# A first mixer whose small tables come through ScalarE's queue into tiles of their own, with constant products while x comes

## Chip, cores and metric

The kernel runs on one core of a Trainium2 chip, in one launch. The metric is the device time of a launch in microseconds: the median of the timed runs. A profiled execution of the kernel before is the source of every row below.

## What is computed

Four transformer layers on 256 tokens of width 1024, in float32, one batch. The first block has a layer with two causal depthwise convolutions as its mixer and a layer with stick-breaking attention, each followed by a mixture of 32 experts; the second block has two attention layers, each with a dense feed-forward part. What the change touches is the mixer of the first layer and what comes before it:

```python
def conv_mixers(x, w_in, conv_a, conv_b_w, conv_b_bias, norm_b_g, norm_b_b, w_out):
    u = jnp.einsum("bsd,de->bse", x, w_in)
    a_b, a_c, a_v, b_val, b_gate = jnp.split(u, [...], axis=-1)
    y_a = a_b * causal_depthwise_conv(a_c * a_v, conv_a)
    g = b_val * jax.nn.sigmoid(b_gate)
    g = causal_depthwise_conv(g, conv_b_w) + conv_b_bias
    y_b = jax.nn.silu(layer_norm(g, norm_b_g, norm_b_b))
    return jnp.einsum("bse,ed->bsd", jnp.concatenate([y_a, y_b], axis=-1), w_out)
...
x = layer_norm(DEEPNORM_ALPHA * x + mix, ln_mix_g[layer], ln_mix_b[layer])
ffn = hierarchical_moe(x, router_group_w[layer], ..., expert_w_up[layer], expert_w_down[layer])
```

## The kernel before

The program is one sequence of instructions per engine, in the order in which the code issues them; nothing reorders them. `T` is TensorE (PE in the rows), `V` VectorE (DVE), `S` ScalarE (ACT), `G` GpSimd (POOL) and `Q` SyncE (SP), which issues the loads of weights.

Weights are taken as items of 1 MB, each a tile of 128 x 2048 floats, in a fixed list: first the nine items of `even_w_in`, then `even_w_out`, then the experts'. `pump` (line 192 on) issues loads on SP's queue as long as a buffer is free; seven buffers belong to the pool `wa`, others are lent by stages. An item is used in two halves. For a product in full precision a half is split into two parts: ScalarE rounds it (`wh`, line 237) and VectorE subtracts (`wl`, line 248); when both halves of an item are split, its buffer is free and `pump` runs again. The two parts lie in pools of four buffers each, so a split can't run more than four halves ahead of TensorE. `mm3` (lines 396 to 399) makes three products of the parts. `tick` after each half runs work that `later` has put off by so many halves.

At the start `load_x` (line 296) and line 303 load x in two pieces of 128 tokens, and item 0 in two pieces between them. Line 202, in `pump`, loads the later items. `conv_mix` (line 540) then does, in this order: it issues the loads of the convolution's rows (lines 551 to 555: three rows of `even_conv_a`, 31 of `even_conv_b_w`, three of one row each) into `fvr`, seven loads of two rows each into `vr` (`vector_loads`, line 324), both of which are parts of one tile `scr`, and four loads for the router (lines 718 to 722); between them `pump` issues items. TensorE turns x piece by piece (`turned`, line 507), ScalarE rounds it (line 579), VectorE subtracts (line 580), both into `xh` and `xl`. Then the units of products begin: the first unit's first half is the opening (line 409), 24 products, whose first eight need only the rounded parts; its second half and all later halves are 24 products at lines 397 to 399. After the first unit (two halves) `vecs` (line 586) turns `fvr`, one half later `vectors` (line 331) turns `vr`. `tap_rows`, `tap_diag`, `shifted` and `conv` make the long convolution out of products.

Loads that SP and ScalarE issue each raise one of eight completion semaphores, DMAHW0 to DMAHW7. The framework hands these out in turn, over the two queues together, and a load that takes a semaphore again waits on its engine until the load that had it before is complete.

Of the kernel before, what the change touches and what calls it, by code (L numbers as in the profile page):

```python
# [10 lines left out]
F32 = mybir.dt.float32  # L11
# [9 lines left out]
SEQ = 256  # L21
# [44 lines left out]
def rows(ap):  # L66
    return ap.rearrange("(k p) n -> p k n", p=128)
# [3 lines left out]
def tile_kernel(ctx: ExitStack, tc: tile.TileContext, A, out, first=0, last=9):  # L71
# [12 lines left out]
    def bank():  # L84
        return psum.tile([128, 512], F32, name="ps", tag="ps")
# [230 lines left out]

    fvec = const.tile([128, 8, 14], F32, name="fvec")

    def vector_loads(vr):
        lo, hi = (0 if first < 4 else 8), (14 if last > 3 else 8)  # L320
        for j, n in enumerate(("ln_mix_g", "ln_mix_b", "ln_ffn_g", "ln_ffn_b", "norm_mix_2", "norm_ffn_2",
                               "norm_ple_2")):
            if lo <= 2 * j < hi:
                Q.dma_start(vr[2 * j:2 * j + 2, :], A[n])
        if lo:
            V.memset(vr[0:8, :], 0.0)

        def go():
            ps = bank()
            for k in range(8):  # L330
                T.transpose(ps[:, k * 14:k * 14 + hi], vr[0:hi, k * 128:(k + 1) * 128], ident[:hi, :hi])
            V.tensor_copy(fvec[:, :, 0:hi], ps[:, 0:112].rearrange("p (k n) -> p k n", k=8)[:, :, 0:hi])
        return go
# [206 lines left out]
    def conv_mix():  # L540


        with tc.tile_pool(name="cm", bufs=1, reuse_waits="tile") as cp:
            wd = [c_tile(F32).rearrange("p (n f) -> p n f", f=32) for _ in range(2)]
            xh, xl = take_c(2)
            scr = cp.tile([128, 2048], F32, name="scr")
            fvr, vr = scr[0:37, 0:512], scr[0:14, 1024:2048]
            yb = scr[:, 1024:2048].rearrange("p (b t) -> p b t", b=4)
            sq = scr[:, 0:1024].rearrange("p (b t) -> p b t", b=4)
            pump(2)  # L550
            Q.dma_start(fvr[0:3, :], A["even_conv_a"][0])
            Q.dma_start(fvr[3:34, :], A["even_conv_b_w"][0])
            Q.dma_start(fvr[34:35, :], A["even_conv_b_bias"])
            Q.dma_start(fvr[35:36, :], A["even_norm_b_g"])
            Q.dma_start(fvr[36:37, :], A["even_norm_b_b"])
            pump(1)
            vectors = vector_loads(vr)
            prep = router_loads(0)
            pump()
            vec = cp.tile([128, 4, 37], F32, name="vec")  # L560
            o512 = cp.tile([128, 128], F32, name="o512")
            G.memset(o512, 1.0 / 512)


            gp = cp.tile([128, 2, 32 + SEQ], F32, name="gp")
            gs = cp.tile([128, 2, 4, 28 + SEQ], F32, name="gs")
            ap = cp.tile([128, 2, 2 + SEQ], F32, name="ap")
            G.memset(gp[:, :, 0:30], 0.0)
            G.memset(gp[:, :, 30 + SEQ:], 0.0)
# [5 lines left out]
            for c in range(2):  # L575
                for kq in range(2):
                    v = turned(c, kq)
                    s = (slice(None), slice(4 * kq, 4 * kq + 4), slice(c * 128, (c + 1) * 128))
                    S.activation(xh[s], v, AF.Copy)
                    V.tensor_tensor(out=xl[s], in0=v, in1=xh[s].bitcast(F32), op=OP.subtract)  # L580
                split_to(c + 1)

            def vecs():
                ps = bank()
# [19 lines left out]

            def shifted():

                for b in range(2):
                    ps = [bank()[:, 0:28 + SEQ] for _ in range(4)]
                    for s in range(4):
                        for c in range(4):  # L610
                            f = slice(32 * c, 32 * c + 32)
                            T.matmul(ps[c][32 * s:32 * s + 32], ident[f, f], gp[f, b, s:s + 28 + SEQ], start=True,
                                     stop=True)
                    for c in range(4):
                        if c % 2:
                            S.activation(gs[:, b, c, :], ps[c], AF.Copy)
                        else:
                            V.tensor_copy(gs[:, b, c, :], ps[c])

            def conv(i):  # L620
                ps = bank()
                for b in range(2):
                    for q in range(8):
                        for c in range(4):
# [23 lines left out]
            nc.scalar.preload_act_table_set("silu_and_others")  # L648


            kept = {}

            def b_sum():
                m = bank()
                for b in range(4):
                    T.matmul(m[:, :256], o512, yb[:, b, :], start=b == 0, stop=b == 3)
                for b in range(4):
                    V.tensor_tensor(out=yb[:, b, :], in0=yb[:, b, :], in1=m[:, :256], op=OP.subtract)
                    S.activation(sq[:, b, :], yb[:, b, :], AF.Square)

            def b_stats():
                p2 = bank()
                for b in range(4):
                    for c in range(2):
                        T.matmul(p2[:, c:c + 1], sq[:, b, c * 128:(c + 1) * 128], o512[:, 0:1],
# [45 lines left out]

    rt = {}

    def router_loads(layer):

        mp = rt["pool"]
        rw = mp.tile([128, 8, 36], F32, name="rw")
        Q.dma_start(rw[:, :, 0:4], rows(A["router_group_w"][layer]))
        Q.dma_start(rw[:, :, 4:36], rows(A["router_expert_w"][layer]))
        lgc = mp.tile([1, 36], F32, name="lgc")  # L720
        Q.dma_start(lgc[:, 0:4], flat(A["router_group_b"][layer], 0, [[0, 1], [1, 4]]))
        Q.dma_start(lgc[:, 4:36], flat(A["router_expert_b"][layer], 0, [[0, 1], [1, 32]]))

        def go():
            ps = bank()
# [1292 lines left out]
```

## Time and profile before

| | us |
|---|---|
| median of 3 runs | 1921.65 |
| lowest and highest | 1921.64, 1921.94 |
| profiled execution | 1918.91 |
| its span | 1917.3 |
| TensorE busy | 1631.0 (85%) |
| VectorE busy | 738.6 (39%) |
| ScalarE busy | 676.8 (35%) |

The span is the time between the first and the last instruction of the profiled execution. TensorE's busy time counts instructions that wait in its pipeline, so it isn't a measure of peak use. In 40 slices of the span the DMA engines are full in two long stretches, the expert stages, and partly idle in the stages with dense products.

### The profile page before, as it was taken

The page shows a single profiled execution, that of the slowest core. Times are in us where ns is not written, and L with a number is a line of the kernel's source. Part 1 is how long each engine was busy: PE and PEld are TensorE (multiplying, and loading weights), DVE is VectorE, ACT ScalarE, POOL GpSimd, SP SyncE. Part 2 cuts the span into 40 slices and gives each one's busy share as a digit, 9 for nine tenths or more (in the row PEclk, how much of TensorE's full clock was granted, in tenths as well). Part 3 has the DMA queues.
Part 4 walks back from the last instruction along what each step waited for, and adds up shares of the span by engine and source line. Part 5 has one row for each costly group of instructions (what it writes and reads, how often), then busy time and mean ns, then how long its engine had stood idle before and what let it go on. Part 6 is the DMA issues. An engine that isn't in the chain of part 4 may idle for free. (4 is left out here: it accounts for less than half of the span.)

```text
span 1917.3 us, 35268 instructions
## 1 busy us (share of the span) xinstructions
PE 1631.0 (85%) x15117; PEld 1228.9 (64%) x15117; DVE 738.6 (39%) x1503; ACT 676.8 (35%) x1297; POOL 122.0 (6%) x126
## 2 busy tenths in 40 slices
PE   8999667677679998767667669999999998999998
PEld 7875323233238985323224227999999996799998
DVE  5551000001005661001001005666656857666557
ACT  4422111111116643111111114655444645654445
POOL 0010000000001000000000002101000412210002
PEclk9999878777789999878778789999999998999999
DMA  9689999999999469999999998545555463145550
GB/s 295 239 306 416 419 418 418 420 419 418 417 406 360 162 257 396 418 419 419 418 419 419 417 419 272 173 138 172 190 194 177 143 202 100 56 156 196 183 176 23
DMA packets 236571, 559.07 MB, mean 292 GB/s; under 512 B 15563, under 2 KB 124938, under 8 KB 236408
## 3 DMA queue, kind: packets, MB, share of 16 engines
q1 hardware_dynamic: 226520, 551.59, 75.2%
q10 hardware_dynamic: 9264, 4.97, 0.9%
q8 instruction: 122, 2.00, 0.4%
q14 instruction: 41, 0.34, 0.0%
q0 software_dynamic: 624, 0.18, 0.0%
HBM read 555.55 MB, written 1.15 MB: 290 GB/s over the span
## 5 line engine op out<-in xcount | busy, mean ns | idle before, releaser
L904 PE MATMUL ps<-w,xg 128*32 128x256 f32 x4096 | 365.0, 496 | 233.3 <-DMA w<-in_expert_w_up_dram 232.1
L904 PEld LDWEIGHTS ps<-w,xg 128*32 128x32 f32 x4096 | 136.1, 132 | 444.2 <-DMA w<-in_expert_w_up_dram 264.1
L248 DVE TENSOR_TENSOR wl<-w,wh 128x1024 fp32r<-128x1024 f32 x255 | 310.1, 1228 | 171.6 <-ACT wh L237 167.4
L237 ACT ACTIVATE wh<-w 128x1024 fp32r<-128x1024 f32 x273 | 283.1, 1051 | 91.5 <-PE ps L398 60.3
L908 DVE TENSOR_TENSOR hs<-hs,ps 128x128 f32<-128x128 f32 x64 | 18.4, 288 | 632.4 <-ACT hs L907 632.4
L397 PE MATMUL ps<-xh,wh 128*128 128x256 f32 (+1 forms) x840 | 237.1, 282 | 0.0
L399 PE MATMUL ps<-xh,wl 128*128 128x256 f32 (+1 forms) x840 | 236.3, 281 | 0.8 <-DVE wl L248 0.8
L398 PE MATMUL ps<-xl,wh 128*128 128x256 f32 (+1 forms) x840 | 236.6, 282 | 0.3 <-DVE xl L1229 0.3
L907 ACT ACTIVATE hs<-ps 128x128 f32<-128x128 f32 x64 | 17.8, 277 | 591.8 <-PE ps L904 587.2
L399 PEld LDWEIGHTS ps<-xh,wl 128*128 128x128 f32 (+1 forms) x840 | 159.2, 190 | 1.2 <-DVE wl L248 1.2
L398 PEld LDWEIGHTS ps<-xl,wh 128*128 128x128 f32 (+1 forms) x840 | 159.2, 190 | 1.1 <-DVE xl L1229 1.1
L397 PEld LDWEIGHTS ps<-xh,wh 128*128 128x128 f32 (+1 forms) x840 | 159.3, 190 | 0.0
L926 PE MATMUL ps<-w,ht 128*32 128x256 f32 x2048 | 142.2, 425 | 0.4 <-DMA w<-in_expert_w_down_dram 0.4
L933 ACT ACTIVATE y<-ps 32x256 f32<-32x256 f32 x256 | 95.8, 374 | 118.5 <-PE ps L926 111.6
L926 PEld LDWEIGHTS ps<-w,ht 128*32 128x32 f32 x2048 | 73.6, 127 | 67.6 <-issue 33.9
L399 PE MATMUL ps<-wh,xl 128*128 128x256 f32 x352 | 100.9, 287 | 4.5 <-DVE xl L1229 4.5
L397 PE MATMUL ps<-wh,xh 128*128 128x256 f32 x352 | 103.1, 293 | 1.5 <-ACT xh L1226 1.5
L248 POOL TENSOR_TENSOR wl<-w,wh 128x1024 fp32r<-128x1024 f32 x18 | 43.4, 2416 | 942.3 <-ACT wh L237 463.4
L398 PE MATMUL ps<-wl,xh 128*128 128x256 f32 x352 | 100.6, 286 | 0.0
L398 PE MATMUL ps<-al,wh 128*128 128x256 f32 x352 | 99.1, 281 | 0.0
L397 PE MATMUL ps<-ah,wh 128*128 128x256 f32 x352 | 99.1, 281 | 0.0
L399 PE MATMUL ps<-ah,wl 128*128 128x256 f32 x352 | 99.0, 281 | 0.0
(400 smaller groups left out, 2756.3 us busy)
## 6 DMA issues: line engine op xcount, KB each, us to landing
w<-in_expert_w_up_dram SPq DMA_DIRECT2D x256, 1024.0 KB
w<-in_expert_w_down_dram SPq DMA_DIRECT2D x128, 1024.0 KB
w<-in_w_ffn_gate_dram SPq DMA_DIRECT2D x22, 1024.0 KB
w<-in_w_ffn_up_dram SPq DMA_DIRECT2D x22, 1024.0 KB
w<-in_w_ffn_down_dram SPq DMA_DIRECT2D x22, 1024.0 KB
w<-in_odd_w_qkv_dram SPq DMA_DIRECT2D x12, 1024.0 KB
w<-in_w_in_ab_dram SPq DMA_DIRECT2D x12, 1024.0 KB
w<-in_w_in_nsa_dram SPq DMA_DIRECT2D x10, 1024.0 KB
```

What stands on the lines that cost most here:

```text
L237: S.activation(hv, src, AF.Copy)
L248: eng.tensor_tensor(out=lv, in0=src, in1=hv.bitcast(F32), op=OP.subtract)
L397: T.matmul(ps, lh, rh, start=start, stop=False, **kw)
L398: T.matmul(ps, lh, rl, start=False, stop=False, **kw)
L399: T.matmul(ps, ll, rh, start=False, stop=stop, **kw)
L904: T.matmul(pu[32 * j:32 * j + 32, 0:256], r, w[:, kk, :, j, :], start=k == 0, stop=k == 7)
L907: S.activation(hs, pu[:, 0:128], AF.Silu)
L908: V.tensor_tensor(out=hs, in0=hs, in1=pu[:, 128:256], op=OP.mult)
L926: T.matmul(pd[32 * c:32 * c + 32, 0:256], hts[e][:, 32 * j:32 * j + 32], w[:, jj, c * 256:(c + 1) * 256], start=j == 0, stop=j == 3)
L933: S.activation(y4s[q][32 * ee:32 * ee + 32, c * 256:(c + 1) * 256], pd[32 * c:32 * c + 32, 0:256], AF.Copy)
```

## The change

The loads of the small tables get an engine as a parameter, ScalarE, and stand together ahead of the first items that `pump` issues; the parts of `scr` become tiles of their own (`yb`, `fvr`, `vr`; `gs` and `sq` take the places of `fvr` and `vr` later on). ScalarE loads the table of the sigmoid once, behind these issues, in place of a first table at once and the sigmoid's later. `warm(n)` issues n products of 128 x 512 on a constant tile: eight before x, three between its two pieces.

```diff
-    def vector_loads(vr):
+    def vector_loads(vr, eng=Q):
...
-                Q.dma_start(vr[2 * j:2 * j + 2, :], A[n])
+                eng.dma_start(vr[2 * j:2 * j + 2, :], A[n])
...
-            scr = cp.tile([128, 2048], F32, name="scr")
-            fvr, vr = scr[0:37, 0:512], scr[0:14, 1024:2048]
-            yb = scr[:, 1024:2048].rearrange("p (b t) -> p b t", b=4)
-            sq = scr[:, 0:1024].rearrange("p (b t) -> p b t", b=4)
-            pump(2)
-            Q.dma_start(fvr[0:3, :], A["even_conv_a"][0])
...
-            Q.dma_start(fvr[36:37, :], A["even_norm_b_b"])
-            pump(1)
-            vectors = vector_loads(vr)
-            prep = router_loads(0)
+            yb = cp.tile([128, 4, SEQ], F32, name="yb")
+            fvr = cp.tile([37, 512], F32, name="fvr", tag="gs")
+            vr = cp.tile([14, D], F32, name="vr", tag="sq")
+            S.dma_start(fvr[0:3, :], A["even_conv_a"][0])
...
+            S.dma_start(fvr[36:37, :], A["even_norm_b_b"])
+            vectors = vector_loads(vr, S)
+            prep = router_loads(0, S)
+            nc.scalar.preload_act_table_set("sigmoid_and_others")
             pump()
+            warm(8)
...
                 split_to(c + 1)
+                if not c:
+                    warm(3)
...
+                gs = kept["gs"] = cp.tile([128, 2, 4, 28 + SEQ], F32, name="gs")
...
+                sq = kept["sq"] = cp.tile([128, 4, SEQ], F32, name="sq")
...
-    def router_loads(layer):
+    def router_loads(layer, eng=Q):
...
-        Q.dma_start(rw[:, :, 0:4], rows(A["router_group_w"][layer]))
-        Q.dma_start(rw[:, :, 4:36], rows(A["router_expert_w"][layer]))
+        eng.dma_start(rw[:, :, 0:4], rows(A["router_group_w"][layer]))
+        eng.dma_start(rw[:, :, 4:36], rows(A["router_expert_w"][layer]))
```

How the instructions stand on ScalarE at the start of the program, before the change; in brackets the semaphores on which an instruction waits (`w<-ps` is the rounding of x into `xh`, `wh<-w` that of a weight half):

```order
L579 ACT_TABLE_LOAD
L579 ACTIVATE w<-ps 128x4x128 [waits PE_49] x2
L237 ACTIVATE wh<-w 128x1024 [waits DMAHW1_49]
L579 ACTIVATE w<-ps 128x4x128 [waits PE_49] x2
L237 ACTIVATE wh<-w 128x1024 [waits DMAHW3_49]
L237 ACTIVATE wh<-w 128x1024 [waits DMAHW4_49]
L237 ACTIVATE wh<-w 128x1024
L237 ACTIVATE wh<-w 128x1024 [waits DMAHW5_49,DVE_49,PE_49]
L640 ACT_TABLE_LOAD
L640 ACTIVATE sg<-ps 128x512 [waits PE_49]
```

ScalarE issues no load here, and the rounding of x follows the first table load. In the changed kernel ScalarE's order is this, from the last loads of norm rows on (ahead of them stand the other eleven small loads):

```order
L324 DMA vr<-in_norm_ple_dram 2x1024 [waits DMAHW2_49]
L719 DMA rw<-in_router_group_w_dram 128x8x4 [waits DMAHW3_49]
L720 DMA rw<-in_router_expert_w_dram 128x8x32 [waits DMAHW4_49]
L722 DMA lgc<-in_router_group_b_dram 1x4 [waits DMAHW6_49]
L723 DMA lgc<-in_router_expert_b_dram 1x32 [waits DMAHW7_49]
L556 ACT_TABLE_LOAD
L578 ACTIVATE w<-ps 128x4x128 [waits PE_49] x2
L237 ACTIVATE wh<-w 128x1024
L578 ACTIVATE w<-ps 128x4x128 [waits PE_49] x2
L237 ACTIVATE wh<-w 128x1024 [waits DMAHW1_49]
L237 ACTIVATE wh<-w 128x1024 x2
L237 ACTIVATE wh<-w 128x1024 [waits DVE_49,PE_49]
```

All sixteen small loads stand ahead of the table load and of the rounding of x; the roundings of items 1 and 2 (the last two rows) have no wait for a load any more.

On SP's queue at the start of the program, before the change (the first `w` loads are the pieces of item 0, then items 1 and 2, and later item 3):

```order
L296 DMA x<-in_x_dram 128x1024
L303 DMA w<-in_even_w_in_dram 128x8x128
L296 DMA x<-in_x_dram 128x1024
L303 DMA w<-in_even_w_in_dram 128x8x128
L202 DMA w<-in_even_w_in_dram 128x8x256 x2
L551 DMA scr<-in_even_conv_a_dram 3x512
L552 DMA scr<-in_even_conv_b_w_dram 31x512
L553 DMA scr<-in_even_conv_b_bias_dram 1x512 [waits DMAHW0_49]
L554 DMA scr<-in_even_norm_b_g_dram 1x512 [waits DMAHW1_49]
L555 DMA scr<-in_even_norm_b_b_dram 1x512 [waits DMAHW2_49]
L202 DMA w<-in_even_w_in_dram 128x8x256 [waits DMAHW3_49]
L324 DMA scr<-in_ln_mix_g_dram 2x1024 [waits DMAHW4_49]
```

The first six loads wait for nothing, and the small loads stand between items 2 and 4. SP's queue in the changed kernel (the loads at line 202 are items 1, 2, 3 and so on):

```order
L296 DMA x<-in_x_dram 128x1024
L303 DMA w<-in_even_w_in_dram 128x8x128
L296 DMA x<-in_x_dram 128x1024
L303 DMA w<-in_even_w_in_dram 128x8x128 [waits DMAHW1_49]
L202 DMA w<-in_even_w_in_dram 128x8x256 [waits DMAHW3_49]
L202 DMA w<-in_even_w_in_dram 128x8x256 [waits DMAHW6_49]
L202 DMA w<-in_even_w_in_dram 128x8x256 [waits DMAHW1_49]
L202 DMA w<-in_even_w_in_dram 128x8x256 [waits DMAHW5_49]
L202 DMA w<-in_even_w_in_dram 128x8x256 [waits DMAHW0_49]
```

The small loads are gone from SP's queue, all nine items follow each other, and from the second piece of item 0 on each load waits for an earlier one, item 1 on DMAHW3 and item 2 on DMAHW6.

## Rows read from the trace of the kernel before

**Rows 1.** The page's head: the span of the profiled execution.

```profile
span 1917.3 us, 35268 instructions
```

**Rows 2.** Two stretches: us, busy time of each engine, granted clock, DMA share, GB/s.

```profile
core 0: us, PE busy (x) PEld busy (x) DVE busy (x) ACT busy (x) POOL busy (x), PEclk, DMA share, GB/s
60.00:80.00 20.00, 20.00 (x233) 16.67 (x233) 7.54 (x14) 5.67 (x11) 1.62 (x1) 1.00 0.50 189
300.00:400.00 100.00, 65.60 (x692) 30.08 (x694) 6.80 (x21) 14.26 (x39) 0.00 (x0) 0.81 1.02 419
```

**Rows 3.** SP's waits, 0 to 150 us: us in total, times, longest.

```profile
SPq L202 <- DVE wl L248: 56.7, 9, 18.2
...
SPq L324 <- DMA w<-in_even_w_in_dram: 2.3, 2, 1.3
```

**Rows 4.** TensorE's weight loads in time: start, us, line, count, idle time before them.

```profile
8.13 1.57 PEld L507 LDWEIGHTS ps<-ident,x 128*128 128x128 f32 x8 [1.77 <-DMA x<-in_x_dram]
9.94 1.79 PEld L409 LDWEIGHTS ps<-w,wh 128*128 128x128 f32 x8 [0.23 <-ACT w L579]
11.61 1.82 PEld L409 LDWEIGHTS ps<-w,wl 128*128 128x128 f32 x8
...
14.68 0.19 PEld L397 LDWEIGHTS ps<-w,wh 128*128 128x128 f32 x1
...
17.36 0.19 PEld L399 LDWEIGHTS ps<-w,wl 128*128 128x128 f32 x1
19.06 0.33 PEld L586 LDWEIGHTS ps<-ident,scr 37*128 37x128 f32 x4 [1.51 <-DMA scr<-in_norm_mix_dram]
...
22.89 0.57 PEld L331 LDWEIGHTS ps<-ident,scr 14*128 14x128 f32 x8 [0.59 <-DMA scr<-in_norm_mix_dram]
```

**Rows 5.** The same view at the opening of the attention stage.

```profile
588.05 1.05 PEld L409 LDWEIGHTS ps<-w,wh 128*128 128x128 f32 x8 [2.39 <-ACT w L1103]
589.04 1.00 PEld L409 LDWEIGHTS ps<-w,wl 128*128 128x128 f32 x8
```

**Rows 6.** ScalarE in time, 0 to 17 us.

```profile
0.91 1.28 ACT L579 ACT_TABLE_LOAD   x1 [0.91 <-PEq L2004]
5.95 0.60 ACT L579 ACTIVATE w<-ps 128x512 fp32r<-128x512 f32 x1 [3.76 <-PE ps L507]
...
9.29 0.60 ACT L579 ACTIVATE w<-ps 128x512 fp32r<-128x512 f32 x1 [0.94 <-PE ps L507]
10.14 0.60 ACT L579 ACTIVATE w<-ps 128x512 fp32r<-128x512 f32 x1 [0.26 <-PE ps L507]
10.64 1.05 ACT L237 ACTIVATE wh<-w 128x1024 fp32r<-128x1024 f32 x1
12.88 2.01 ACT L237 ACTIVATE wh<-w 128x1024 fp32r<-128x1024 f32 x2 [1.20 <-DMA w<-in_even_w_in_dram]
15.98 1.06 ACT L237 ACTIVATE wh<-w 128x1024 fp32r<-128x1024 f32 x1 [1.08 <-DMA w<-in_even_w_in_dram]
```

**Rows 7.** SP's queue in time, 12 to 24 us: start and duration of an issue.

```profile
12.88 1.68 SPq L324 DMA_DIRECT2D scr<-in_ln_mix_g_dram  x1
15.88 0.23 SPq L324 DMA_DIRECT2D scr<-in_ln_mix_b_dram  x1
...
22.53 0.43 SPq L721 DMA_DIRECT2D lgc<-in_router_group_b_dram  x1
23.01 0.25 SPq L722 DMA_DIRECT2D lgc<-in_router_expert_b_dram  x1
23.30 14.04 SPq L202 DMA_DIRECT2D w<-in_even_w_in_dram  x6
```

**Rows 8.** A stretch by engines, columns as in rows 2.

```profile
19.50:29.30 9.80, 9.38 (x83) 9.05 (x82) 8.22 (x15) 4.04 (x10) 0.00 (x0) 1.00 0.65 172
```

**Rows 9.** Stretches of half a microsecond by engines, columns as in rows 2.

```profile
22.50:23.00 0.50, 0.08 (x3) 0.11 (x2) 0.00 (x0) 0.50 (x1) 0.00 (x0) 1.00 0.59 18
23.00:23.50 0.50, 0.50 (x9) 0.47 (x9) 0.00 (x0) 0.50 (x2) 0.00 (x0) 1.00 1.14 114
23.50:24.00 0.50, 0.50 (x5) 0.50 (x5) 0.38 (x2) 0.50 (x1) 0.00 (x0) 1.00 1.17 192
```

More of the change, by code (lines that the diff above doesn't have):

```diff
@@ L545, in conv_mix @@
             xh, xl = take_c(2)
-            scr = cp.tile([128, 2048], F32, name="scr")
-            fvr, vr = scr[0:37, 0:512], scr[0:14, 1024:2048]
-            yb = scr[:, 1024:2048].rearrange("p (b t) -> p b t", b=4)
-            sq = scr[:, 0:1024].rearrange("p (b t) -> p b t", b=4)
-            pump(2)
-            Q.dma_start(fvr[0:3, :], A["even_conv_a"][0])
-            Q.dma_start(fvr[3:34, :], A["even_conv_b_w"][0])
-            Q.dma_start(fvr[34:35, :], A["even_conv_b_bias"])
-            Q.dma_start(fvr[35:36, :], A["even_norm_b_g"])
-            Q.dma_start(fvr[36:37, :], A["even_norm_b_b"])
-            pump(1)
-            vectors = vector_loads(vr)
-            prep = router_loads(0)
+            yb = cp.tile([128, 4, SEQ], F32, name="yb")
+            fvr = cp.tile([37, 512], F32, name="fvr", tag="gs")
+            vr = cp.tile([14, D], F32, name="vr", tag="sq")
+            S.dma_start(fvr[0:3, :], A["even_conv_a"][0])
+            S.dma_start(fvr[3:34, :], A["even_conv_b_w"][0])
+            S.dma_start(fvr[34:35, :], A["even_conv_b_bias"])
+            S.dma_start(fvr[35:36, :], A["even_norm_b_g"])
+            S.dma_start(fvr[36:37, :], A["even_norm_b_b"])
+            vectors = vector_loads(vr, S)
+            prep = router_loads(0, S)
+            nc.scalar.preload_act_table_set("sigmoid_and_others")
             pump()
+            warm(8)
             vec = cp.tile([128, 4, 37], F32, name="vec")
@@ L565, in conv_mix @@
             gp = cp.tile([128, 2, 32 + SEQ], F32, name="gp")
-            gs = cp.tile([128, 2, 4, 28 + SEQ], F32, name="gs")
+            kept = {}
             ap = cp.tile([128, 2, 2 + SEQ], F32, name="ap")
@@ L620, in conv @@
             def conv(i):
-                ps = bank()
+                ps, gs = bank(), kept["gs"]
                 for b in range(2):
@@ L648, in conv_mix @@
             nc.scalar.preload_act_table_set("silu_and_others")
-            kept = {}
             def b_sum():
                 m = bank()
+                sq = kept["sq"] = cp.tile([128, 4, SEQ], F32, name="sq")
                 for b in range(4):
@@ L661, in b_stats @@
             def b_stats():
-                p2 = bank()
+                p2, sq = bank(), kept["sq"]
                 for b in range(4):
@@ L712, in tile_kernel @@
     rt = {}
-    def router_loads(layer):
+    def router_loads(layer, eng=Q):
         mp = rt["pool"]
         rw = mp.tile([128, 8, 36], F32, name="rw")
-        Q.dma_start(rw[:, :, 0:4], rows(A["router_group_w"][layer]))
-        Q.dma_start(rw[:, :, 4:36], rows(A["router_expert_w"][layer]))
+        eng.dma_start(rw[:, :, 0:4], rows(A["router_group_w"][layer]))
+        eng.dma_start(rw[:, :, 4:36], rows(A["router_expert_w"][layer]))
         lgc = mp.tile([1, 36], F32, name="lgc")
-        Q.dma_start(lgc[:, 0:4], flat(A["router_group_b"][layer], 0, [[0, 1], [1, 4]]))
-        Q.dma_start(lgc[:, 4:36], flat(A["router_expert_b"][layer], 0, [[0, 1], [1, 32]]))
+        eng.dma_start(lgc[:, 0:4], flat(A["router_group_b"][layer], 0, [[0, 1], [1, 4]]))
+        eng.dma_start(lgc[:, 4:36], flat(A["router_expert_b"][layer], 0, [[0, 1], [1, 32]]))
         def go():
```

## The prediction

> **What bounds the kernel now.** The profiled execution took 1918.91 us, of which its span is 1917.3 us [rows 1]; the median of the three timed runs is 1921.65 us, 2.74 us (0.14%) more. The sum below is a difference in the span, and I add it to the median. A difference under 0.2%, 3.8 us, can't be told from no change by a measurement of this kernel.
>
> I read the stretch table first, then the starts of the first 24 us engine by engine, since the whole change lies there. In the expert stages the DMA engines are full: share 1.02 and 419 GB/s from 300 to 400 us, with TensorE busy for two thirds of the time. In the first mixer it is the other way: from 60 to 80 us TensorE is busy throughout and the DMA engines half the time [rows 2]. Why the transfers pause there is in SP's waits up to 150 us: nine weight loads waited 56.7 us in all for VectorE's subtraction at line 248, which frees the weight buffer [rows 3]. So in the mixer TensorE's order of work sets when buffers come free, and these set when the expert weights can be fetched. A delay of TensorE at the start goes through to the end one for one, as long as the stream of weights stays limited by buffers there.
>
> Next, TensorE's first 24 us [rows 4]. It turns the second half of x at 8.13 us, when that half has landed. At 9.94 us it begins the 24 products of line 409 (the opening), which need ScalarE's rounded copy of x. They last until 14.68, 4.74 us, and the second half of the unit ends at 17.48. Then it waits 1.51 us for the small table (the releaser is named as the last load into the shared tile `scr`; what it needs are the five convolution rows), and at 22.89 another 0.59 us for the norm rows. These are the two waits that early small tables can take away. The weight loads in the opening start every (11.61 - 9.94) / 8 = 0.209 us, in the next half every (17.36 - 14.68) / 23 = 0.117 us [rows 4]: 1.2 against 2.4 GHz in effect, though the column of the granted clock shows 1.00 there too. The same opening in the attention stage, with constant products running just ahead of it, starts eight in 0.99 us [rows 5]: full speed.
>
> Now ScalarE [rows 6]. It loads a table at 0.91 us, then is free, and rounds the first quarter of x at 5.95 us, at once when TensorE has turned it. All later work of the opening hangs on this ScalarE chain.
>
> **The change part by part.** The 16 small loads leave SP's queue and stand at the head of ScalarE's, ahead of its table load and of all its roundings (the order of ScalarE in the section on the change). What each of the 16 waits for decides everything. A load takes one of eight completion semaphores in turn and first waits for the load that had it before. SP already pays for this: its norm loads at 12.88 and 15.88 us waited for weight tiles, 2.3 us in all [rows 3, 7]; these are the moments at which items 1 and 2 landed, since ScalarE's rounding of those items starts at 12.88 and 15.98 [rows 6]. After the change SP's and ScalarE's loads take the semaphores alternately, and the rows of the order show who follows whom: SP's items 1 and 2 wait for DMAHW3 and DMAHW6 and take them; ScalarE's `router_group_w` then waits for DMAHW3 and `router_group_b` for DMAHW6. So ScalarE can't pass its sixteen issues before weight items 1 and 2, 1 MB each, have landed. That no wait for these two items is left at ScalarE's later roundings of them says the same: it has waited already. Behind the waiting issue stand ScalarE's table load and the rounding of x; behind these VectorE's `xl`, and TensorE's opening.
>
> When does item 2 land? Before: 15.88 us [rows 7], behind 2 MB of x and item 0 and 1 MB of item 1, 3.00 us after item 1. These bytes still go first on SP's queue. SP's item 1 now waits for the first half of item 0, and item 2 for the second half of x, but both come well before the transfers ahead of them are done, so I see no gap. Added to the traffic are 37 rows of 2 KB and 14 rows of 4 KB, 130 KB, which at the 1 MB in 3.00 us are 0.4 us, and part of the router tables: 2048 pieces of 16 and 128 bytes, which before filled the DMA engines from 22.5 us to 24.0, about 1.5 us [rows 9]. `router_group_w` is issued when item 1 has landed, beside item 2, so they share the engines. Item 2 thus lands between 15.9 (none of it matters) and 18.0 us (all does); I take 16.9, nearer to the half since only part of the router pieces can come ahead of it.
>
> From there, with durations of before. ScalarE issues `router_group_b` and `router_expert_b`: SP took from 22.53 to 23.26, 0.73 us [rows 7]; I have no issue on ScalarE in this trace and take SP's. The table load is 1.28 us [rows 6], and with 0.1 us for the signal rounding starts 2.1 us after item 2, at 19.0 us. Then two quarters of x at 0.50 us pitch (10.14 to 10.64), a weight half at 0.96 us (two took 2.01 with the last one's tail), and the third quarter, whose 0.65 us up to TensorE's start (9.29 to 9.94) come on top: 1.96 + 0.65 = 2.6 us [rows 4, 6]. TensorE opens at 21.6 us where it opened at 9.94: **+11.7 us**, between +10.7 and +12.8 with the ends for item 2.
>
> The products on constants (eight before the first half of x, three before the second) run while TensorE would wait for x anyway. Should they delay the turning of x by a microsecond, nothing follows, since ScalarE takes the turned x only at 19 us; that is their cover, and for the same reason their use is lost: TensorE stands idle for ten microseconds between the turned x and the opening. All at the higher level, the opening lasts 24 x 0.117 = 2.8 us, a gain of 1.9. At the lower level through the opening and through the next half: 0.3 + 24 x (0.209 - 0.117) = +2.5. Before, the lower level lasted for most of the opening although TensorE had already worked from 8.13 us [rows 4]; with no work ahead I take **+0.6 us**, a little longer at the lower level. By the Trainium skill, "TensorE: Matmul & The Clock Gate", Part 1, the array's clock falls back to 1.2 GHz after an idle time and rises with activity; that is the slow start I took, and the higher level would make the sum 2.5 us smaller. No row here shows the level after such a gap in this place.
>
> Gains on TensorE's path: the waits of 1.51 and 0.59 us [rows 4] go, since the convolution and norm rows land while ScalarE is blocked: **-2.1 us**. What is late next there? VectorE's chain from the small table to the shifted copies of the convolution: in the 9.8 us from 19.5 to 29.3 VectorE was busy for 8.2 [rows 8]. With 0.6 us less of waiting 9.2 us are left for it, so it still fits; I count nothing.
>
> Costs of nothing: the second table load, once ahead of the sigmoid, goes; it was off TensorE's path. The separate tiles for the rows, `yb`, `gs` and `sq` only change which buffer is waited for. SP loses 16 issues, and its items 4 and later can start some 7 us earlier than at 23.30 [rows 7]; TensorE never waited for one of these in the mixer, and the buffers then run full earlier and wait for the same VectorE releases [rows 3]. The cover is that wait; if it were gone, the earlier stream would be a gain (second rival).
>
> Sum: +11.7 + 0.6 - 2.1 = **+10.2 us**, span 1927.5 and time 1921.65 + 10.2 = **1931.9 us**. Ends: 10.7 - 1.9 - 2.1 = +6.7 (1928.3) and 12.8 + 2.5 - 2.1 = +13.2 (1934.9).
>
> **The rivals.** First, the change does what it says: ScalarE isn't held, since the small loads pass before x lands. Then the opening still begins at 9.94 but runs at the higher level, at most -1.9 us, and the waits of 2.1 us go: 1917.6 us. It needs the last router loads to be issued before 5.95 us. For it: fourteen of the sixteen wait for nothing or for small rows. Against: items 1 and 2 can't land in 6 us when the same bytes took until 15.88. The Trainium skill, "DMA: Bandwidth & Descriptors", Rules for kernel authors, advises to issue a load early, compute, and wait late; that is this rival's course, and the trace agrees only for SP, whose queue holds no computing. Chance 0.09.
>
> Second, the stream of weights sets the end and not TensorE: the hole from 18 to 24.5 us closes and the late opening is swallowed, some -6.5 us, 1915 us. It decides if the buffers are never the limit. The half-idle DMA engines from 60 to 80 us [rows 2] and SP's 56.7 us [rows 3] speak against it. Chance 0.04; with only part of the delay swallowed it would come out as no change, 0.03.
>
> Third, dearer: the router's small pieces and the small rows slow item 2 beyond 18 us (each microsecond costs one), or an issue on ScalarE takes 1.7 us, as SP's did at 12.88 [rows 7]: 1935 to 1938. Chance 0.08.
>
> **How the numbers follow.** The forecast has 0.76. Its own span is 1928.3 to 1934.9; with a little of the dearer case the range from 1927.5 to 1936.0 holds some 8 in 10. Slower by over 0.2% is the forecast and the third rival, 0.84; faster the first and second, 0.13; the same 0.03.
>
> **What would show it.** Right: in the trace after, ScalarE does nothing between its first issues and 18 to 20 us but wait, and the releaser of the router issues is a load of `even_w_in`; the table load stands at 17 to 19 us; line 409 starts near 21.6; the wait ahead of the transposes of `fvr` is gone; SP's weights run without a hole. From 60 us on everything stands some 10 us later. Wrong: ScalarE rounds x at 6 us (first rival), the opening is late but the first expert's products aren't (second), or ScalarE starts after 20 us (third).

## The result and the profile after

The changed kernel takes 1935.89 us, the median of four runs (1933.72 to 1938.5), where the kernel before took 1921.64 in the same comparison. The ratio is 1.0075, 95% interval 1.0057 to 1.0092: slower by 14.4 us, between 11.0 and 17.7. The forecast was +10.2 us and 1931.9, the range ended at 1936.0. The direction, the place and the mechanism were right; the size was 4 us too small, and the steps that were mis-sized are told below.

The profiled execution of the changed kernel took 1938.5 us, the highest of the four; its span is to be read beside [rows 1].

```profile
span 1936.9 us, 35282 instructions
```

ScalarE in time, 0 to 26 us, of the changed kernel: start, duration, engine (ACTq is its queue of issues), line, operation, count, and the idle time before it with what ended it. It answers to [rows 6].

```profile
2.84 0.28 ACTq L324 DMA_DIRECT2D vr<-in_ln_mix_g_dram  x1
7.80 0.24 ACTq L324 DMA_DIRECT2D vr<-in_ln_mix_b_dram  x1
...
9.00 0.26 ACTq L324 DMA_DIRECT2D vr<-in_norm_ffn_dram  x1
12.56 0.24 ACTq L324 DMA_DIRECT2D vr<-in_norm_ple_dram  x1
16.38 0.42 ACTq L719 DMA_DIRECT2D rw<-in_router_group_w_dram  x1
16.84 0.72 ACTq L720 DMA_DIRECT2D rw<-in_router_expert_w_dram  x1
19.53 1.31 ACTq L722 DMA_DIRECT2D lgc<-in_router_group_b_dram  x1
20.88 0.64 ACTq L723 DMA_DIRECT2D lgc<-in_router_expert_b_dram  x1
21.55 1.28 ACT L556 ACT_TABLE_LOAD   x1 [21.55 <-DMA lgc<-in_router_group_b_dram]
22.84 1.08 ACT L578 ACTIVATE w<-ps 128x512 fp32r<-128x512 f32 x2
```

The reader sees four holds in the row of issues: until 7.80, 12.56, 16.38 and 19.53 us. The last two are those of the prediction: the order of the instructions puts `router_group_w` behind weight item 1 and `router_group_b` behind item 2 on their semaphores. ScalarE computes nothing until 22.84 us, where before it rounded the first quarter of x at 5.95 [rows 6]. The profile names `lgc` as the releaser of the table load, which is only the last of the loads that were issued ahead of it; what counts is the start of each issue.

TensorE's weight loads in time, changed kernel, columns as in [rows 4]; line 587 is the transpose of the convolution rows (586 before), and line 614 makes the shifted copies of the convolution's input.

```profile
10.87 1.49 PEld L507 LDWEIGHTS ps<-ident,x 128*128 128x128 f32 x8 [4.67 <-DMA x<-in_x_dram]
25.41 1.78 PEld L409 LDWEIGHTS ps<-w,wh 128*128 128x128 f32 x8 [13.04 <-ACT w L578]
27.07 1.82 PEld L409 LDWEIGHTS ps<-w,wl 128*128 128x128 f32 x8
28.78 1.82 PEld L409 LDWEIGHTS ps<-w,wh 128*128 128x128 f32 x8
33.96 0.33 PEld L587 LDWEIGHTS ps<-ident,fvr 37*128 37x128 f32 x4
37.35 0.57 PEld L331 LDWEIGHTS ps<-ident,vr 14*128 14x128 f32 x8
43.75 0.84 PEld L614 LDWEIGHTS ps<-gp,ident 32*32 32x32 f32 x38
```

The shifted copies start at this time in the kernel before (the same view):

```profile
29.29 0.84 PEld L612 LDWEIGHTS ps<-gp,ident 32*32 32x32 f32 x38
```

The opening comes at 25.41 instead of 9.94 us [rows 4], 15.47 us later, after 13.04 us of idle TensorE that ScalarE ended. The 1.51 and 0.59 us of [rows 4] are gone: the rows of lines 587 and 331 have no bracket. By the shifted copies the whole program is 43.75 - 29.29 = 14.46 us late, and nothing takes it back. In the attention stage the opening stood at 588.05 us [rows 5]; in the changed kernel:

```profile
602.59 1.06 PEld L409 LDWEIGHTS ps<-w,wh 128*128 128x128 f32 x8 [2.39 <-ACT w L1104]
```

That is 14.54 us later, after the mixer and the stretches of experts. The second rival (the stream of weights sets the end and swallows the delay) is out.

What sits on top of 14.5 us in the profiled execution (19.6 us between the spans) is no part of the change's mechanism: this execution lies 2.6 us above its median, and the profiled one of the kernel before 2.7 us under its own. Two stretches of the changed kernel (us, busy time of the engines, granted clock, DMA share, GB/s, as in [rows 2]):

```profile
1151.00:1172.00 21.00, 13.52 (x145) 5.57 (x145) 0.87 (x3) 2.06 (x6) 0.00 (x0) 0.67 1.03 404
1529.60:1553.00 23.40, 19.21 (x116) 18.97 (x116) 16.65 (x23) 10.30 (x17) 10.89 (x14) 0.73 0.41 120
```

and the same work in the kernel before, 14.5 and 15.9 us earlier:

```profile
1136.50:1157.50 21.00, 14.95 (x166) 6.27 (x166) 1.16 (x4) 3.55 (x10) 0.00 (x0) 0.76 1.01 398
1513.70:1537.10 23.40, 19.17 (x149) 18.74 (x148) 16.63 (x23) 10.43 (x18) 10.88 (x14) 0.93 0.43 131
```

At these two late places the granted clock was longer at the lower level in the changed kernel's execution (0.67 and 0.73, a mean of 1.2 and 2.4 GHz over the stretch) than in the one before (0.76 and 0.93). The instructions of VectorE, matched one by one between the two traces, are 14.4 us late from 50 to 160 us, 14.5 from 560 to 740, 16 from 1160 and 20 from 1540; in the expert stages between these the lateness moves between 13 and 17. A second execution of the same program (the first experiment) lost less at the second place, so these places vary from one execution to the next; why the clock stays low there longer in one than in another stays open.

### The profile page after: what moved, and what is told of

Read it like the earlier page. It is cut to its first block, busy times and chain, and to the rows that moved or that the text cites. A ratio compares the mean times of both kernels' runs of the same rounds, so it can differ in the third digit from the quotient of the medians.

```text
span 1936.9 us, 35282 instructions
## 1 busy us (share of the span) xinstructions
PE 1637.2 (85%) x15128; PEld 1231.9 (64%) x15128; DVE 738.0 (38%) x1503; ACT 675.0 (35%) x1296; POOL 122.0 (6%) x126
```

## The experiments

Every ratio is to the kernel before on the same chip, with its 95% interval. All of these kernels compute the whole result. The table puts three things side by side: where the opening (line 409) starts, how much later than before the shifted copies start (29.29 us there), and the difference in time that the ratio gives on 1921.6 us.

| kernel | opening, us | shifted copies against before, us | ratio | time against before, us |
|---|---|---|---|---|
| before | 9.94 | 0 | 1 | 0 |
| changed | 25.41 | +14.46 | 1.0075 [1.0057, 1.0092] | +14.4 |
| again | 25.06 | +13.99 | 1.0072 [1.0058, 1.0085] | +13.8 |
| no_warm | 25.62 | +13.86 | 1.0071 [1.0055, 1.0086] | +13.6 |
| rows16 | 24.00 | +12.16 | 1.0069 [1.0053, 1.0084] | +13.3 |
| router_sp | 16.71 | +4.44 | 1.0032 [1.0021, 1.0043] | +6.1 |
| hold2 | 18.68 | +6.97 | 1.0036 [1.0023, 1.0050] | +6.9 |
| act_late | 9.26 | +16.39 | 1.0092 [1.0072, 1.0111] | +17.7 |
| sp_q | 9.05 | +1.91 | 1.0009 [1.0000, 1.0019] | +1.7 |
| pool_q | 10.44 | -1.74 | 1.0006 [0.9997, 1.0016] | +1.2 |
| pool_16 | 9.79 | +0.39 | 1.0010 [1.0001, 1.0019] | +1.9 |
| pool_router | 10.04 | -1.31 | 0.9998 [0.9988, 1.0007] | -0.4 |

**The changed kernel a second time.** No edit; the run tells what belongs to the program and what to one execution.

> The changed kernel once more, with more runs. Theory: ScalarE is held by the waits of its router issues, so line 409 opens near 25.4 us and the shift against the kernel before is about 14.4 us from 44 us up to the end of the second expert stage; what comes on top differs from execution to execution, by how long TensorE stays at its lower clock at two late places (near 1155 to 1173 and 1542 to 1554 us in the profile), so the times fall into groups near 1934 and 1938 with all opening times alike. Rival: the opening itself differs between executions, by 4 us.

Measured: 1934.78 us, median of five, 1.0072 [1.0058, 1.0085]. Its opening stands at 25.06 us and its shifted copies at 43.28, 0.47 us sooner than in the first trace; the late places gave less. From 1520 to 1560 us its granted clock is 0.96, as it is before, while the first trace of the changed kernel has 0.83 there. So the loss of some 14 us at the start is in both traces, and what comes late is not. The five times (1933.0 to 1936.16) don't fall into the two groups that I had expected.

**The loads on another queue.** The small loads keep their place ahead of item 1's and their own tiles, but GpSimd issues them, behind its constants; ScalarE issues nothing.

```diff
-            S.dma_start(fvr[0:3, :], A["even_conv_a"][0])
...
-            vectors = vector_loads(vr, S)
-            prep = router_loads(0, S)
...
             G.memset(wv, 0.0)
+            G.dma_start(fvr[0:3, :], A["even_conv_a"][0])
...
+            vectors = vector_loads(vr, G)
+            prep = router_loads(0, G)
```

> The changed kernel with the sixteen small loads on GpSimd's queue, which has completion semaphores of its own, behind GpSimd's constants; ScalarE issues none. Theory (the semaphores that ScalarE's loads share with the weights hold it): ScalarE rounds x near 6 us, line 409 opens near 10 us at the higher clock, no wait for the small tables: 1.9 + 2.1 us less than before, about 1917.6. Rival (the small pieces slow x and items 1 and 2 whatever queue they come from): line 409 opens 2 us or more late, 1922 or more.

Measured: 1921.79 us, 1.0006 [0.9997, 1.0016]. The loss is gone. TensorE's weight loads of this kernel:

```profile
10.44 1.02 PEld L409 LDWEIGHTS ps<-w,wh 128*128 128x128 f32 x8 [0.49 <-ACT w L578]
16.26 0.32 PEld L587 LDWEIGHTS ps<-ident,fvr 37*128 37x128 f32 x4
27.55 0.86 PEld L614 LDWEIGHTS ps<-gp,ident 32*32 32x32 f32 x38 [1.60 <-issue]
```

and of VectorE ahead of the copies:

```profile
18.56 1.22 DVE L248 TENSOR_TENSOR wl<-w,wh 128x1024 fp32r<-128x1024 f32 x1 [0.99 <-ACT wh L237]
...
26.75 0.68 DVE L644 TENSOR_TENSOR gp<-sg,ps 128x512 f32<-128x512 f32 x1
```

The opening runs at the higher level (1.02 us for eight, where [rows 4] has 1.79), the wait of 1.51 us is gone, and at the shifted copies the kernel is 1.74 us ahead. There TensorE waits 1.60 us, for `gp`, which VectorE finishes at 27.43: its chain behind item 2 is late next, which I had counted at nothing. The 1.7 us stand in the trace up to 160 us, and at the opening of the attention stage 0.4 of them are left (587.65 against 588.05 us). Beyond the mixer one trace against another says little: between 160 and 700 us ten of the eleven other traces, this one among them, lose 0.8 to 2.3 us against the one trace of the kernel before. In the time the gain doesn't show, whose interval reaches from -0.6 to +3.1 us; where it goes isn't settled.

**The loads at their old place.** SP issues the small loads between the items again; the tiles of their own, the one table load and the constant products stay.

```diff
-            S.dma_start(fvr[0:3, :], A["even_conv_a"][0])
...
+            pump(2)
+            Q.dma_start(fvr[0:3, :], A["even_conv_a"][0])
...
+            pump(1)
-            vectors = vector_loads(vr, S)
-            prep = router_loads(0, S)
+            vectors = vector_loads(vr)
+            prep = router_loads(0)
```

> The changed kernel with the sixteen small loads back at their places on SP's queue; tiles of their own, the early table load and the constant products stay. Theory: all of the loss is the queue; the opening at the higher clock gains up to 1.9 us, the tiles of their own let the convolution rows be turned without waiting for the norm rows, up to 1.5 us: 1918 to 1920. Rival (the tiles or the constant products cost): slower than before, 1922 or more.

Measured: 1923.47 us, 1.0009 [1.0000, 1.0019]: the loss goes with the queue, as the theory has it, but the gain that I expected isn't there. The row tells why:

```profile
19.19 0.50 PEld L589 LDWEIGHTS ps<-ident,fvr 37*128 37x128 f32 x4 [4.44 <-DMA vr<-in_norm_mix_dram]
```

The convolution rows themselves come at about 19 us here, and an earlier opening only makes TensorE wait longer for them, 4.44 us instead of 1.51. The shared tile `scr` was never the reason for the wait ahead of the transposes. The 1.9 us by which the copies come later than in the kernel before are the price of that longer wait: in it the granted clock fell, and the half behind the transposes runs at the lower level.

```profile
17.50:24.00 6.50, 4.78 (x24) 4.74 (x25) 2.79 (x10) 3.10 (x9) 0.00 (x0) 0.50 0.35 64
```

From the transposes of the convolution rows to those of the norm rows it is 24.80 - 19.19 = 5.61 us, where [rows 4] has 22.89 - 19.06 = 3.83 with a wait of 0.59 in it.

**The wait alone.** The kernel before, with one instruction added: ScalarE reads sixteen columns of item 2 ahead of its rounding of x. No load moves.

```diff
             pump()
+            held = cp.tile([128, 16], F32, name="held")
+            S.activation(held, raw[2][:, 0:16], AF.Copy)
```

> The kernel before, with one small ScalarE operation ahead of its rounding of x that reads weight item 2, so that ScalarE waits until that item has landed; nothing else is changed. Theory: this wait alone makes the loss. The rounding starts near 16.2 us in place of 5.95, line 409 opens near 18.8 in place of 9.94, +8.9, with up to 1 us more at the lower clock and the waits of 2.1 us for the small tables gone: the shift is +7 to +8 us from there on, 1928.5 to 1930 (up to 4 us more where TensorE stays longer at its lower clock late in the program). Rival (later stages swallow such a delay): under 1925.

Measured: 1927.58 us, 1.0036 [1.0023, 1.0050]. ScalarE and TensorE in time:

```profile
16.00 0.22 ACT L561 ACTIVATE held<-w 128x16 f32<-128x16 f32 x1 [13.80 <-DMA w<-in_even_w_in_dram]
16.13 1.07 ACT L581 ACTIVATE w<-ps 128x512 fp32r<-128x512 f32 x2
```

```profile
18.68 1.78 PEld L409 LDWEIGHTS ps<-w,wh 128*128 128x128 f32 x8 [8.85 <-ACT w L581]
26.48 0.32 PEld L588 LDWEIGHTS ps<-ident,scr 37*128 37x128 f32 x4
36.26 0.84 PEld L614 LDWEIGHTS ps<-gp,ident 32*32 32x32 f32 x38
```

Holding ScalarE until item 2 has landed opens line 409 at 18.68, 8.74 us late; the waits of 2.1 us are covered, the shift at the copies is 6.97 us, and the time is 6.9 us longer. The delay goes through to the end one for one within the interval (4.4 to 9.6 us), and this one wait makes half of the loss, in a kernel that has nothing else of the change.

**The router's issues moved back.** The changed kernel, with the four router loads back on SP's queue behind item 3. ScalarE then waits for nothing on item 1 or 2 ahead of the rounding of x.

```diff
             vectors = vector_loads(vr, S)
-            prep = router_loads(0, S)
             nc.scalar.preload_act_table_set("sigmoid_and_others")
+            pump(3)
+            prep = router_loads(0)
             pump()
```

> The changed kernel with the four router loads alone back on SP's queue, behind weight item 3. ScalarE's remaining twelve loads wait for nothing or for small rows. Theory: the two waits for weight items are gone, but the norm rows still wait for the convolution rows, which land late: ScalarE's last issue near 12.5 us, the rounding of x near 14.1, line 409 opens near 16.7 (+6.8), 1 us longer at the lower clock, 2.1 us of waits gone: +5.5, some 9 us less than the changed kernel. Rival (any load on ScalarE's queue costs the whole 14 us, or none does): the opening at 25, or at 10.

Measured: 1926.36 us, 1.0032 [1.0021, 1.0043]. ScalarE's last issue and what follows:

```profile
12.58 0.24 ACTq L324 DMA_DIRECT2D vr<-in_norm_ple_dram  x1
12.85 1.28 ACT L555 ACT_TABLE_LOAD   x1 [12.85 <-DMA vr<-in_ln_mix_b_dram]
14.14 1.08 ACT L579 ACTIVATE w<-ps 128x512 fp32r<-128x512 f32 x2
```

Up to here its times are those of the changed kernel (12.58 against 12.56), so the two holds behind items 1 and 2 and the router issues cost 22.84 - 14.14 = 8.70 us of ScalarE's time and 10.0 us at the copies (14.46 - 4.44); in the time the two kernels are 8.3 us apart (14.4 - 6.1). The holds at 7.80 and 12.56, which I had not priced at all, alone make the kernel 4.4 us late. In the full change they lie inside the longer wait.

**The 31 rows in two pieces.** In the changed kernel SP's items come later than I had them, and between 9 and 11 us the DMA engines are nearly idle. Two stretches of it, columns as in [rows 2]:

```profile
9.00:10.00 1.00, 0.00 (x0) 0.00 (x0) 0.00 (x0) 0.00 (x0) 0.00 (x0) 1.00 0.20 64
10.00:11.00 1.00, 0.12 (x1) 0.13 (x2) 0.00 (x0) 0.00 (x0) 0.00 (x0) 1.00 0.29 89
```

The suspicion fell on the load of 31 convolution rows of 2 KB. In the kernel before it is issued at 9.40 us, ahead of item 3 (11.51 us). From 18.5 to 22 us the DMA engines are nearly idle there, yet item 3 is still coming: of the 79 packets of this stretch 52 have between 512 B and 2 KB, and only items have such pieces (1 KB). They follow one another until 20.96 us. The packets of the stretch, and its first half microsecond:

```profile
DMA packets 79, 0.10 MB, mean 29 GB/s; under 512 B 15, under 2 KB 67, under 8 KB 79
```

```profile
18.50:19.00 0.50, 0.00 (x0) 0.00 (x0) 0.00 (x0) 0.45 (x1) 0.00 (x0) 1.00 0.11 33
```

A share of 0.11 is one or two engines of sixteen: an engine has fallen behind the others. In the changed kernel ScalarE's first hold, until 7.80 us, is for the landing of the 31 rows, 6.3 us after their issue at 1.52. The packets of the trace show them one after another from 4.28 to 7.29 us, 3.0 us for 62 KB. ScalarE's queue (q10) from 4.2 to 7.4 us: packets, MB, share of sixteen engines.

```profile
q10 hardware_dynamic: 34, 0.07, 5.8%
```

That is 0.93 of one engine. After it the last rows of the second half of x end one by one too, eight of them between 9.06 and 10.24 us, in the hole. The Trainium skill, "DMA: Bandwidth & Descriptors", section "Why a DMA increments its semaphore by 16 and not by 1", says that a transfer is spread over the largest number of engines, up to 16, that divides its slowest dimension; 31 rows would go to one engine. The row of q10 agrees. The experiment loads them as 16 and 15 rows:

```diff
-            S.dma_start(fvr[3:34, :], A["even_conv_b_w"][0])
+            S.dma_start(fvr[3:19, :], A["even_conv_b_w"][0, 0:16])
+            S.dma_start(fvr[19:34, :], A["even_conv_b_w"][0, 16:31])
```

> The changed kernel with the 31 rows of the convolution's taps loaded in two pieces of 16 and 15 rows; ScalarE's loads still wait for weight items 1 and 2. Theory (the one piece of 31 rows runs on a single DMA engine, and the pieces of x and of item 0 that this engine carries land 2 to 3 us late, so that SP, which waits for them, leaves the DMA engines idle from 9 to 11 us): the gap closes, item 2 lands near 17 in place of 19.5 us, line 409 opens near 22.5 to 23.4 in place of 25.2: 2 to 2.5 us less than the changed kernel. Rival (the gap comes from SP's waits alone, whatever the small loads are): line 409 opens near 25 as before.

Measured: 1933.46 us, 1.0069 [1.0053, 1.0084]. The hole is closed (9 to 11 us):

```profile
9.00:10.00 1.00, 0.49 (x5) 0.25 (x3) 0.00 (x0) 0.00 (x0) 0.00 (x0) 1.00 0.99 294
10.00:11.00 1.00, 0.00 (x0) 0.00 (x0) 0.00 (x0) 0.00 (x0) 0.00 (x0) 1.00 1.07 326
```

SP issues item 1 at 6.83 us instead of 9.45, TensorE turns the second half of x at 8.39 instead of 10.87, and the issue that waits for item 2 starts at 17.65 instead of 19.53. So the hole was this one load. The opening at 24.00 us is later than the 22.5 to 23.4 that I expected. ScalarE's rows behind item 2:

```profile
17.65 0.40 ACTq L721 DMA_DIRECT2D rw<-in_router_expert_w_dram  x1
18.09 1.71 ACTq L723 DMA_DIRECT2D lgc<-in_router_group_b_dram  x1
19.84 0.26 ACTq L724 DMA_DIRECT2D lgc<-in_router_expert_b_dram  x1
20.14 1.28 ACT L557 ACT_TABLE_LOAD   x1 [20.14 <-DMA lgc<-in_router_group_b_dram]
```

Of the 1.88 us only 1.41 arrive at the opening, since one load more on the queue turns the semaphores by one and three issues (2.5 us up to the table load) stand behind item 2 instead of two. The copies come 2.3 us sooner than in the changed kernel; the two ratios overlap, so in the time the gain is not shown.

**Without the products on constants.** The two calls of `warm` are left out, which are no part of the result.

```diff
-            warm(8)
...
-                if not c:
-                    warm(3)
```

> The changed kernel without the constant products. Theory: these lie ten microseconds ahead of the opening and have no use there; nothing depends on them, so the opening starts near 25.2 us at the lower clock and the time is that of the changed kernel within 0.1%. Rival (they delay the turning of x, or hold the clock up a little at the opening): a difference of 1 us or more at the first long convolution (43.5 us).

Measured: 1934.41 us, 1.0071 [1.0055, 1.0086], with the opening at 25.62 us and the same slow eight loads of 1.78 us. The products are of no use where they stand, as forecast: TensorE idles for 13 us between them and the opening.

**Behind the roundings, on ScalarE's queue.** If only the place ahead of x costs, the same loads behind the roundings of x and of items 0 and 1 should cost little.

```diff
-            S.dma_start(fvr[0:3, :], A["even_conv_a"][0])
...
-            prep = router_loads(0, S)
             nc.scalar.preload_act_table_set("sigmoid_and_others")
...
                 if not c:
                     warm(3)
+            S.dma_start(fvr[0:3, :], A["even_conv_a"][0])
...
+            prep = router_loads(0, S)
```

> The changed kernel with one difference: the sixteen small loads stay on ScalarE's queue and keep their own tiles, but stand behind ScalarE's roundings of x and of items 0 and 1 instead of ahead of them. If it is the place ahead of the rounding that costs, and not the use of ScalarE's queue as such, the opening (line 409) starts near 9.5 to 10.5 us as it did before, instead of 25.4; the small loads are then issued from about 13 to 20 us, so the convolution rows land late and the wait ahead of their transposes stays or grows by 1 to 4 us, and the router issues hold the rounding of item 2 until it has landed, which that rounding needs anyway: 1921 to 1927. If ScalarE's queue itself is what is dear (long issues, holds in the queue wherever they stand), most of the loss stays: 1931 or more.

Measured: 1938.33 us, 1.0092 [1.0072, 1.0111]: my theory missed here, and the lesson is wider than I had it. ScalarE's queue of this kernel:

```profile
12.67 0.23 ACTq L581 DMA_DIRECT2D fvr<-in_even_norm_b_b_dram  x1
16.70 0.24 ACTq L324 DMA_DIRECT2D vr<-in_ln_mix_g_dram  x1
21.48 0.24 ACTq L324 DMA_DIRECT2D vr<-in_ln_mix_b_dram  x1
...
24.50 0.24 ACTq L324 DMA_DIRECT2D vr<-in_norm_mix_dram  x1
...
31.64 0.59 ACTq L723 DMA_DIRECT2D lgc<-in_router_group_b_dram  x1
32.27 0.41 ACTq L724 DMA_DIRECT2D lgc<-in_router_expert_b_dram  x1
32.73 2.95 ACT L237 ACTIVATE wh<-w 128x1024 fp32r<-128x1024 f32 x3 [22.01 <-DMA w<-in_even_w_in_dram]
```

The opening is where it should be, at 9.26 us and at the higher level. But SP now runs further ahead with its items, so the sixteen loads follow more of them on the shared semaphores: they are held at 12.67, 16.70, 21.48, 24.50 and later, and the rounding of the next items, which stands behind them, starts at 32.73 us. TensorE waits for that rounding:

```profile
33.84 0.29 PEld L397 LDWEIGHTS ps<-w,wh 128*128 128x128 f32 x1 [13.80 <-ACT wh L237]
```

It is not only the place ahead of x that is dear: at both places tried, the loads on the queue of a computing engine hold its computing while another queue streams large loads on the same semaphores.

**Two variants of the GpSimd queue.** The first adds the split of the 31 rows (the diff of rows16 on that kernel), the second puts the four router loads behind item 3 on SP's queue (the diff of router_sp on it).

> The small loads on GpSimd's queue as in the second run, with the 31 rows of taps in two pieces of 16 and 15. Theory (one DMA engine carries the single piece and delays x): x's second half is turned near 8 in place of 9.1 us, item 2 lands earlier, and line 409 opens near 9.3 in place of 10.4 us; at the first long convolution 0.5 to 1.5 us earlier than with one piece, 1919 to 1920.5, under the kernel before by less than can be told. Rival (no change from the pieces): line 409 at 10.4.

> The run with the small loads on GpSimd's queue, but with the four router loads back on SP's queue behind weight item 3. There the opening was 1.9 us better than before, yet what is late next was VectorE's chain behind item 2, which ended at 27.55 us at the transposes of the shifted copies. If item 2 is held up by the router's small pieces, it lands up to 1 us sooner here, the transposes start at 26.5 to 27.3 us (before: 29.29) and the time is 1919.5 to 1921.5. If those pieces do not hold it up, the transposes stay at 27.5 and the time at 1921 to 1922.5. Either way the gain at 50 us is at most 2.8 us, so the time can't fall below 1918.5.

Measured: 1922.86 us, 1.0010 [1.0001, 1.0019], and 1921.28 us, 0.9998 [0.9988, 1.0007]. With the split rows the opening is sooner (9.79 against 10.44), but ScalarE waits for item 2 until 19.60, and the copies come at 29.68 us; this trace is of an execution 7 us above its median, and I draw no more from it than that the gain of 0.5 to 1.5 us that I expected of the split did not show. With the router loads on SP the copies stand at 27.98, no sooner than 27.55, and ScalarE rounds item 2 at 17.88 as against 17.47: the router's pieces were not what held item 2 there. The kernels on GpSimd's queue can't be told from the kernel before, and no version here beats it.

## Why the prediction was right in kind and too small in size

**The bound** held. A delay at the start goes through one for one: the table's columns of copies and of time agree within the intervals for every delay of 1.9 us and more (1.9, 4.4, 7.0, 12.2, 14.5 and 16.4); these intervals are 4 to 7 us wide. The shift of 14.5 us still stands at 602 us. For a gain it isn't shown: the copies 1.74 us sooner on GpSimd's queue brought no shorter time.

**The hold on ScalarE** held, and for the reason given. The issues of the router tables start at 16.38 and 19.53 us; moving those four loads away takes 10.0 us off the delay at the copies and 8.3 off the time, and the wait for item 2 alone, put into the kernel before, costs 6.9 us.

**When item 2 lands** is the step that failed first: 19.53 us against 16.9, outside the 15.9 to 18.0 that I gave it, **+2.6 us**. The sentence that failed is "so I see no gap". I had counted the bytes that stand ahead of item 2 and not what the 31 rows do to the piece of every other load that goes to their DMA engine; with the chain of semaphores on SP, the late pieces delay the issue of item 1 to 9.45 us, and the hole from 9 to 11 us follows. With the rows split, item 2 lands at 17.65, inside the bounds: 1.9 of the 2.6 us are this load. The other 0.7 no run takes apart, but the router's pieces are at most 0.15 of it: item 2 lands 19.53 - 16.38 = 3.15 us after item 1, where it was 3.00 before. The trace before could have shown it: [rows 9] gives the share of the DMA engines in halves of a microsecond, and I never asked for the stretch from 18.5 us on, in which one engine is left with item 3.

**The issues on ScalarE** are the second: from 19.53 us to the table load's start at 21.55 it is 2.02 us, where I took 0.73 from SP and 0.1 for the signal, **+1.2 us**. One issue took 1.31 us (1.71 with the rows split). I had this as a part of the third rival, from SP's 1.68 us in [rows 7], and gave it too little; the measured time lies at the lower end of that rival's 1935 to 1938. From the rounding to the opening it was 25.41 - 22.84 = 2.57 us, against 2.6.

**The clock** at the opening is the third. From the opening to the transposes of the convolution rows it is 33.96 - 25.41 = 8.55 us, against 19.06 - 1.51 - 9.94 = 7.61 before [rows 4], +0.94, and up to the copies another 0.15: 1.09 against the 0.6 that I took, **+0.5 us**. All 24 loads of the opening run at 0.21 us pitch here, and the granted clock reads 0.50 through the empty stretch ahead of it:

```profile
15.00:20.00 5.00, 0.00 (x0) 0.00 (x0) 0.00 (x0) 0.00 (x0) 0.00 (x0) 0.50 1.06 350
```

It rose at 31.49 us, 6.1 us after the opening began. The trace of the kernel before has its first record of the clock at 14.24 us, a rise to 1.00 at 4.3 us after the opening began; the column counts what lies ahead of the first record as 1.00. So the 1.00 that I set against the pitch of 0.209 us in the prediction is no measured clock: by the pitch it was the lower level. The bound of +2.5 held, but the size of this term goes with the execution: from the opening to the copies it is 18.34 us here and 18.22 in the second trace, 17.53 without the products and 17.45 with the split rows, against 29.29 - 9.94 - 2.10 = 17.25 before.

**The gains** were right: both waits are gone, -2.1 us, and the constant products do nothing, as the run without them shows. What I said is late next, VectorE's chain, "still fits" behind a late opening; on GpSimd's queue, with the opening at 10.44, it no longer does and costs 1.6 us.

The measured terms, 15.47 + 1.09 - 2.10, are the 14.46 us at the shifted copies by the way they are taken; the time, measured apart from them, is 14.4 us longer. The upper end of my sum, +13.2, was too low because no term of it had a loss on SP's side; with the third rival the range ended at 1936.0, where the ratio on the median gives 1936.1.

**The rivals.** The first (ScalarE isn't held) is refuted by the first rows above, and the run on GpSimd's queue shows what it would have given at best: no difference that the time shows, not -4 us. The second is refuted at 602 us. The third was the right one in size, and both its causes came: item 2 landed after 18 us, by the small rows (1.9 us by the 31 on one engine) and hardly by the router's pieces; and one issue took 1.31 us. I gave it 0.08.

## What to carry to other kernels

Count a load's wait for its completion semaphore as an instruction of the engine that issues it: on an engine that computes, sixteen cheap loads cost here as much as the landing of the 1 MB loads that another queue had put on the same semaphores, and the order of instructions lists each such wait before anything runs. A small load whose number of rows divides badly is not small to its neighbours; look at the DMA engines' share in the stretch where it comes in before you call a stretch of transfers free of gaps. And a wait that disappears from a profile is worth only what the next chain leaves of it, here 1.7 us at one place and nothing in the time. A wait that moves ahead of products can also take TensorE's clock down: with the loads at their old place, 2.9 us more of waiting cost another 1.8 us at the lower level behind it.

## What the runs showed of the hardware that I had not expected

An issue of a small load on ScalarE takes 0.24 to 0.33 us in most rows, but 1.31 and 1.71 us for a load of four numbers beside SP's stream; on GpSimd the same kinds of issue took 0.48 to 0.96 us. One load of 31 rows, 62 KB, moved the landing of the second half of x by 2.5 us (turned at 10.87 against 8.39) and the issue of a 1 MB item by 2.6 us (9.45 against 6.83). And in the changed kernel the granted clock fell at 11.01 us, after TensorE had waited 4.67 us for x, and stayed at 0.50 through 13 idle microseconds and the opening until 31.49 us; with the loads on GpSimd's queue, where TensorE had waited 2.35 us for x, it was 1.00 from 6.33 us on, and the opening took 1.02 us for eight loads instead of 1.78.
